# A tiled softmax: eight rows of the sixth chunk loaded on ScalarE's DMA queue, and all row scaling on VectorE one row at a time

## The chip, the cores and the metric

The kernel runs on one core of one Trainium2 chip. The metric is device time in microseconds of that core. Three runs of the kernel before took 161.74 to 161.76 us, with a median of 161.75 us.

## The reference

The input `x` is 16 x 1024 rows of 512 float32 values. The output is a softmax over each row with temperature 0.5:

```python
x_scaled = x / 0.5
x_max = np.max(x_scaled, axis=-1, keepdims=True)
exp_x = np.exp(x_scaled - x_max)
return (exp_x / np.sum(exp_x, axis=-1, keepdims=True)).astype(np.float32)
```

That is 33.55 MB to read from device memory and 33.55 MB to write back.

## The kernel before

The 16,384 rows are cut into eight chunks of 2048 rows. A chunk is one tile `xt` of 128 partitions with 16 rows each, so each partition holds 16 x 512 floats (32 KB, contiguous in device memory), and a chunk is 4 MB. Six buffers hold six chunks. Chunks 6 and 7 (counted from 0, as in the code) reuse the buffers of chunks 0 and 1. Everything is done in place.

A chunk is worked on as one or more blocks (`BLOCKS`): chunk 0 in blocks of 4, 4 and 8 rows, chunk 7 in two of 8 rows, the others whole. This gives eleven blocks. For one block the steps are:

- `load` (line 68): a DMA on SyncE's (SP's) queue. Chunk 0 comes in two parts (1 MB and 3 MB), chunks 1 to 6 whole, and chunk 7 without its last row per partition.
- `shift` (lines 77 and 81): VectorE takes the negated maximum of every row in one reduction and doubles it; this is the bias.
- `exponentials` (line 108): ScalarE takes each row's exponential with that bias in one activation, and the sum of the row beside it (`accum_out`, a second instruction in the trace).
- `scale_vector` (lines 125 and 127): VectorE takes the reciprocals of the sums and multiplies seven eighths of the rows by them in one broadcast tensor-tensor product (14 of 16 rows; of a 4-row block, all).
- `scale_scalar` (line 138): ScalarE multiplies the remaining rows one by one with a copy activation (two rows of a whole chunk, one of an 8-row block).
- `store` (line 148): a DMA on ScalarE's queue writes the whole chunk (4 MB).

The order on each engine is the order in which the program issues it, written out by hand in the loop at the end. Step `i` issues the exponentials of block `i+1`, then the scaling of block `i`, then the load and the maximum of block `i+2`, then the store of block `i`. Chunk 1 is an exception: its last two exponentials come behind the store of chunk 0 (`cut`). The last row per partition of chunk 7 is loaded by GpSimd (`load_last_row`, lines 90 and 97) once the exponentials of chunk 5 have reached row 10.

A DMA is carried by 16 DMA engines. Each takes 8 of the 128 partitions, so a whole-chunk transfer is 8 packets of 32 KB on each engine. The trace calls SP's queue q1, ScalarE's q10, GpSimd's q0, and the one that fetches instructions q14.

Of the kernel before, what the change touches and what calls it, by code (L numbers as in the profile page):

```python
# [1 line left out]

# [4 lines left out]


@with_exitstack
def kernel(  # L10
    ctx: ExitStack,
    tc: tile.TileContext,
    x: bass.AP,
    out: bass.AP,
):
    nc = tc.nc
    fp32 = mybir.dt.float32
    P = nc.NUM_PARTITIONS
    AX = mybir.AxisListType.X
    EXP = mybir.ActivationFunctionType.Exp  # L20
    COPY = mybir.ActivationFunctionType.Copy
    MAX = mybir.AluOpType.max

    D = x.shape[-1]
    xf = x.flatten_outer_dims()
    of = out.flatten_outer_dims()
    N = xf.shape[0]

    G = 16
    C = N // (P * G)
    assert C * P * G == N
    xr = xf.rearrange("(c p g) d -> c p g d", p=P, g=G)
    outr = of.rearrange("(c p g) d -> c p g d", p=P, g=G)
    WHOLE = [(0, G)]
    LOADS = [[(0, 4), (4, G)]] + [WHOLE] * 6 + [[(0, G - 1)]]
    BLOCKS = [[(0, 4), (4, 8), (8, G)]] + [WHOLE] * 6 + [[(0, 8), (8, G)]]
    STORES = [WHOLE] * 8  # L40
    BMAX = 16
    BUFS = 6

    data = ctx.enter_context(tc.tile_pool(name="data", bufs=BUFS))
    stats = ctx.enter_context(tc.tile_pool(name="stats", bufs=6))

    ctx.enter_context(tc.manual_schedule())


    warm = stats.tile([P, 1], fp32, name="warm", bufs=1)  # L50
    nc.vector.memset(warm, 0.0)  # L51
    nc.scalar.activation(out=warm, in_=warm, func=EXP)  # L52

    chunks = {}
    blocks = [(c, lo, hi) for c in range(C) for lo, hi in BLOCKS[c]]
    n = len(blocks)
    biases, sums, recips = {}, {}, {}

    finished = []

    def load(c):
        if c < BUFS:
            chunks[c] = data.tile([P, G, D], fp32, name="xt")
        else:
            chunks[c] = chunks[c - BUFS]
        xt = chunks[c]
        for lo, hi in LOADS[c]:
            part = nc.sync.dma_start(out=xt[:, lo:hi, :], in_=xr[c][:, lo:hi, :])  # L68
            finished.append(part.ins.name)

    def shift(i):
        c, lo, hi = blocks[i]
        if c not in chunks:
            load(c)
        b = hi - lo
        negmax = stats.tile([P, BMAX], fp32, name="negmax")
        nc.vector.tensor_reduce(  # L77
            negmax[:, 0:b], chunks[c][:, lo:hi, :], axis=AX, op=MAX, negate=True
        )
        biases[i] = stats.tile([P, BMAX], fp32, name="bias")  # L80
        nc.vector.tensor_scalar_mul(biases[i][:, 0:b], negmax[:, 0:b], 2.0)  # L81

    def load_last_row(signal):
        seen = stats.tile([P, 1], fp32, name="seen", bufs=1)
        copied = nc.gpsimd.tensor_copy(out=seen, in_=signal)  # L90
        finished.append(copied.ins.name)
        c = C - 1
        halves = "p (h d) -> p h d"
        to = chunks[c - BUFS][:, G - 1, :].rearrange(halves, h=2)
        of_ = xr[c][:, G - 1, :].rearrange(halves, h=2)
        for p0, p1 in ((P - 2, P), (0, P - 2)):
            part = nc.gpsimd.dma_start(  # L97
                out=to[p0:p1], in_=of_[p0:p1], max_dma_last_dim=2 * D
            )
            finished.append(part.ins.name)  # L100

    def exponentials(i, rows):
        c, lo, hi = blocks[i]
        if i not in sums:
            sums[i] = stats.tile([P, BMAX], fp32, name="sums")
        for g in rows:
            row = chunks[c][:, lo + g, :]
            nc.scalar.activation(  # L108
                out=row,
                in_=row,  # L110
                func=EXP,
                bias=biases[i][:, g : g + 1],
                scale=2.0,
                accum_out=sums[i][:, g : g + 1],
            )
            if c == BUFS - 1 and g == 10:
                load_last_row(sums[i][:, g : g + 1])


    def scale_vector(i):  # L120
        c, lo, hi = blocks[i]
        b = hi - lo
        k = b - b // 8
        recips[i] = stats.tile([P, BMAX], fp32, name="recip")
        nc.vector.reciprocal(recips[i][:, 0:b], sums[i][:, 0:b])  # L125
        rows = chunks[c][:, lo : lo + k, :]
        last = nc.vector.tensor_mul(  # L127
            rows, rows, recips[i][:, 0:k].unsqueeze(2).broadcast_to((P, k, D))
        )
        if i == n - 1:  # L130
            finished.append(last.ins.name)

    def scale_scalar(i):
        c, lo, hi = blocks[i]
        b = hi - lo
        for g in range(b - b // 8, b):
            row = chunks[c][:, lo + g, :]
            last = nc.scalar.activation(  # L138
                out=row, in_=row, func=COPY, scale=recips[i][:, g : g + 1]
            )  # L140
            if i == n - 1:
                finished.append(last.ins.name)

    def store(i):
        c, _, end = blocks[i]
        for lo, hi in STORES[c]:
            if hi == end:
                part = nc.scalar.dma_start(
                    out=outr[c][:, lo:hi, :], in_=chunks[c][:, lo:hi, :]
                )  # L150
                if c < C - 1:
                    finished.append(part.ins.name)

    shift(0)
    shift(1)

    def rows(i):
        c, lo, hi = blocks[i]
        cut = hi - lo - (2 if c == 1 else 0)
        return range(cut), range(cut, hi - lo)  # L160

    exponentials(0, rows(0)[0])
    for i in range(n):
        if i + 1 < n:
            exponentials(i + 1, rows(i + 1)[0])
        scale_vector(i)
        scale_scalar(i)
        if i + 2 < n:
            shift(i + 2)
        store(i)  # L170
        if i + 1 < n:
            exponentials(i + 1, rows(i + 1)[1])

    seen = nc.sync.nop()
    info = mybir.DependencyInfo(
        mybir.DependencyClass.Sync, mybir.DependencyReason.DATA
    )
    for name in finished:
        tc.add_manual_dep(seen.ins, name, info, reason="leaves one wait for the end")


# [1 line left out]
_INS = ['x']  # L183
_OUTS = [((16, 1024, 512), 'float32')]


# [23 lines left out]
```

## Time and profile before

| What | Value |
|---|---|
| Runs, median (lowest to highest) | 161.75 us (161.74 to 161.76) |
| Span of the profiled execution | 160.5 us |
| VectorE (DVE) busy | 134.6 us, 84% of the span |
| ScalarE (ACT) busy | 102.2 us, 64% of the span |
| Moved by DMA | 67.13 MB, mean 418 GB/s |
| Time of SP's and ScalarE's packets, as a share of the 16 DMA engines' span | 49.3% and 48.4% |
| First and last store issued | at 44.1 and 147.5 us |

The profiled execution lists its span, and no total of its own beside it. The runs' median lies 1.24 us above the span, which is what lies around the span: start and end of the program. Times in the trace count from the start of the span. Busy shares are averages; the share in one stretch is read from the slices and windows of the profile. A packet is put down to the slice in which it starts, so a single short slice can show more or less than the DMA engines moved in it.

### The profile page before, as it was taken

The numbers are of one execution on the slowest core, as the hardware profiler recorded it, in microseconds if no ns is written. First come the engines' busy times: TensorE is split into PE (matmuls) and PEld (weight loads), VectorE is DVE, ScalarE is ACT, GpSimd is POOL, SyncE is SP. The second block draws the span as 40 slices with busy tenths as digits, with TensorE's granted clock in tenths as the row PEclk, the third lists the DMA queues.
The fourth block names the chain that finished last, engine by engine and source line by source line (L and its number), as shares of the span: only waits on it lengthen the run. The fifth ranks groups of instructions, "written<-read, shape, count | busy, mean of one in ns | idle before, by whom it ended". The sixth has DMA issues, their size and how long they took to land.

```text
span 160.5 us, 411 instructions
## 1 busy us (share of the span) xinstructions
DVE 134.6 (84%) x45; ACT 102.2 (64%) x273; POOL 1.9 (1%) x7
## 2 busy tenths in 40 slices
DVE  0607999999999999999999999999999999957000
ACT  3071549069989963998199909991899891790000
POOL 0000000000000000000000000030000000000000
DMA  5999999999989999999999999989999999999994
GB/s 184 470 408 498 400 392 457 457 392 402 506 269 425 490 392 400 506 400 392 490 425 392 474 434 392 490 383 483 422 450 400 400 465 441 392 457 449 400 441 204
DMA packets 2578, 67.13 MB, mean 418 GB/s; under 512 B 328, under 2 KB 328, under 8 KB 400
## 3 DMA queue, kind: packets, MB, share of 16 engines
q1 hardware_dynamic: 1296, 33.29, 49.3%
q10 hardware_dynamic: 1152, 33.55, 48.4%
q0 software_dynamic: 128, 0.26, 0.4%
q14 instruction: 2, 0.02, 0.0%
HBM read 33.55 MB, written 33.55 MB: 418 GB/s over the span
## 4 chain that ended last, share of the span: by engine, by line
DVE 75%; DMA 7%; issue 5%; ACT 3%; SPq 0%
DVE negmax L77 42%; DVE xt L127 31%; DMA xt<-in_x_dram 7%; ACT xt L108 3%; DVE bias L81 1%; DVE recip L125 1%; SPq L68 0%
## 5 line engine op out<-in xcount | busy, mean ns | idle before, releaser
L108 ACT ACTIVATE xt<-xt,bias 128x512 f32<-128x512 f32 x128 | 90.4, 708 | 41.5 <-DVE bias L81 40.6
L77 DVE TENSOR_REDUCE negmax<-xt 128x16 f32<-128x8192 f32 (+2 forms) x11 | 69.9, 6352 | 9.4 <-DMA xt<-in_x_dram 9.4
L127 DVE TENSOR_TENSOR xt<-xt,recip 128x7168 f32<-128x7168 f32 (+2 forms) x11 | 62.0, 5637 | 0.4
L108 ACT ACTIVATION_READ_ACCUMULATOR xt<-xt,bias 128x1 f32 x128 | 23.9, 187 | 0.0
L138 ACT ACTIVATE xt<-xt,recip 128x512 f32<-128x512 f32 x15 | 9.9, 706 | 0.0
L125 DVE RECIPROCAL recip<-sums 128x16 f32<-128x16 f32 (+2 forms) x11 | 2.4, 218 | 1.8 <-ACT xt L108 1.8
L81 DVE TENSOR_SCALAR bias<-negmax 128x16 f32<-128x16 f32 (+2 forms) x11 | 1.9, 173 | 0.4
L52 ACT ACT_TABLE_LOAD x1 | 1.3, 1283 | 0.7 <-PEq L194 0.7
L97 POOL DMA_DIRECT2D xt<-in_x_dram x2 | 1.5, 741 | 0.5 <-issue 0.5
L90 POOL COPY seen<-sums 128x1 f32<-128x1 f32 x1 | 0.2, 184 | 103.6 <-ACT xt L108 103.6
L51 DVE MEMSET warm<- 128x1 f32 x1 | 0.1, 59 | 0.8 <-PEq L194 0.8
L52 ACT ACTIVATE warm<-warm 128x1 f32<-128x1 f32 x1 | 0.2, 202 | 0.0
L194 POOL MEMSET const-float32-0.0<- 128x1 f32 x1 | 0.1, 93 | 0.2 <-issue 0.2
L194 POOL MEMSET const-bfloat16-1.0<- 128x1 bf16 x1 | 0.1, 95 | 0.0
L194 POOL MEMSET const-uint8-127<- 128x1 uint8 x1 | 0.1, 95 | 0.0
L194 POOL MEMSET const-float32-1.0<- 128x1 f32 x1 | 0.1, 93 | 0.0
## 6 DMA issues: line engine op xcount, KB each, us to landing
out_dram<-xt ACTq DMA_DIRECT2D x8, 4096.0 KB, 23.1
xt<-in_x_dram SPq DMA_DIRECT2D x6, 4096.0 KB, 34.8
xt<-in_x_dram SPq DMA_DIRECT2D x1, 3840.0 KB, 27.8
xt<-in_x_dram SPq DMA_DIRECT2D x1, 3072.0 KB, 11.6
xt<-in_x_dram SPq DMA_DIRECT2D x1, 1024.0 KB, 4.8
xt<-in_x_dram POOLq DMA_DIRECT2D x1, 252.0 KB, 15.4
xt<-in_x_dram POOLq DMA_DIRECT2D x1, 4.0 KB, 9.1
```

The costliest lines, as they stand in the source:

```text
L51: nc.vector.memset(warm, 0.0)
L52: nc.scalar.activation(out=warm, in_=warm, func=EXP)
L77: nc.vector.tensor_reduce(negmax[:, 0:b], chunks[c][:, lo:hi, :], axis=AX, op=MAX, negate=True)
L81: nc.vector.tensor_scalar_mul(biases[i][:, 0:b], negmax[:, 0:b], 2.0)
L90: copied = nc.gpsimd.tensor_copy(out=seen, in_=signal)
L97: part = nc.gpsimd.dma_start(out=to[p0:p1], in_=of_[p0:p1], max_dma_last_dim=2 * D)
L108: nc.scalar.activation(out=row, in_=row, func=EXP, bias=biases[i][:, g : g + 1], scale=2.0, accum_out=sums[i][:, g : g + 1],)
L125: nc.vector.reciprocal(recips[i][:, 0:b], sums[i][:, 0:b])
L127: last = nc.vector.tensor_mul(rows, rows, recips[i][:, 0:k].unsqueeze(2).broadcast_to((P, k, D)))
L138: last = nc.scalar.activation(out=row, in_=row, func=COPY, scale=recips[i][:, g : g + 1])
L194: nc = _bacc.Bacc("TRN2", target_bir_lowering=False, num_devices=1)
```

## The change

There are three edits.

First, directly behind the table load and the warm-up activation, ScalarE issues a load of rows 0 to 7 of chunk 5 (the sixth) on its own queue, ahead of all stores. `max_dma_last_dim` cuts each partition's 16 KB into four pieces of two rows (4 KB). SP's queue then loads only rows 8 to 15 of that chunk.

Second, `scale_scalar` is gone. VectorE scales every row with a tensor-scalar product of its own (128 x 512), with the row's reciprocal as the scalar.

Third, the store of chunk 0 is issued after 12 of the 16 exponentials of chunk 1, not after 14.

```diff
-    LOADS = [[(0, 4), (4, G)]] + [WHOLE] * 6 + [[(0, G - 1)]]
+    SLOW = 8
+    LOADS = [[(0, 4), (4, G)]] + [WHOLE] * 4 + [[(SLOW, G)], WHOLE, [(0, G - 1)]]
...
+    def load_slowly(c):
+        chunks[c] = data.tile([P, G, D], fp32, name="xt")
+        part = nc.scalar.dma_start(
+            out=chunks[c][:, 0:SLOW, :],
+            in_=xr[c][:, 0:SLOW, :],
+            max_dma_last_dim=2 * 4 * D,
+        )
+        finished.append(part.ins.name)
+
+    load_slowly(BUFS - 1)
...
     def load(c):
-        if c < BUFS:
+        if c in chunks:
+            pass
+        elif c < BUFS:
             chunks[c] = data.tile([P, G, D], fp32, name="xt")
...
-        if c not in chunks:
+        if lo == 0:
             load(c)
...
-    def scale_vector(i):
+    def scale(i):
         c, lo, hi = blocks[i]
         b = hi - lo
-        k = b - b // 8
         recips[i] = stats.tile([P, BMAX], fp32, name="recip")
         nc.vector.reciprocal(recips[i][:, 0:b], sums[i][:, 0:b])
-        rows = chunks[c][:, lo : lo + k, :]
-        last = nc.vector.tensor_mul(
-            rows, rows, recips[i][:, 0:k].unsqueeze(2).broadcast_to((P, k, D))
-        )
+        for g in range(b):
+            row = chunks[c][:, lo + g, :]
+            last = nc.vector.tensor_scalar_mul(row, row, recips[i][:, g : g + 1])
         if i == n - 1:
             finished.append(last.ins.name)
-
-    def scale_scalar(i):
...
-        cut = hi - lo - (2 if c == 1 else 0)
+        cut = hi - lo - (4 if c == 1 else 0)
         return range(cut), range(cut, hi - lo)
...
-        scale_vector(i)
-        scale_scalar(i)
+        scale(i)
```

In the changed program's order, SP's load of the rest of chunk 5 waits for the semaphore of ScalarE's load of its first rows, and the loads of chunks 6 and 7 stand behind it on SP. The exponentials of chunk 5 wait for both of these loads.

More of the change, by code (lines that the diff above doesn't have):

```diff
@@ L20 @@
     EXP = mybir.ActivationFunctionType.Exp
-    COPY = mybir.ActivationFunctionType.Copy
     MAX = mybir.AluOpType.max
@@ L54 @@
     chunks = {}
+    finished = []
+    def load_slowly(c):
[7 more added lines that the diff above has]
+    load_slowly(BUFS - 1)
     blocks = [(c, lo, hi) for c in range(C) for lo, hi in BLOCKS[c]]
@@ L57 @@
     biases, sums, recips = {}, {}, {}
-    finished = []
     def load(c):
-        if c < BUFS:
+        if c in chunks:
+            pass
+        elif c < BUFS:
             chunks[c] = data.tile([P, G, D], fp32, name="xt")
@@ L117, in exponentials @@
                 load_last_row(sums[i][:, g : g + 1])
-    def scale_vector(i):
+    def scale(i):
         c, lo, hi = blocks[i]
         b = hi - lo
-        k = b - b // 8
         recips[i] = stats.tile([P, BMAX], fp32, name="recip")
         nc.vector.reciprocal(recips[i][:, 0:b], sums[i][:, 0:b])
-        rows = chunks[c][:, lo : lo + k, :]
-        last = nc.vector.tensor_mul(
-            rows, rows, recips[i][:, 0:k].unsqueeze(2).broadcast_to((P, k, D))
-        )
+        for g in range(b):
+            row = chunks[c][:, lo + g, :]
+            last = nc.vector.tensor_scalar_mul(row, row, recips[i][:, g : g + 1])
         if i == n - 1:
             finished.append(last.ins.name)
-    def scale_scalar(i):
[L134 to L142, printed above, removed]
     def store(i):
```

## The prediction

> **What bounds the kernel now.** I read the chain of waits first, and it misleads: it blames VectorE.
>
> ```profile
> span 160.5 us, 411 instructions
> DVE 134.6 (84%) x45; ACT 102.2 (64%) x273; POOL 1.9 (1%) x7
> DVE 75%; DMA 7%; issue 5%; ACT 3%; SPq 0%
> ```
>
> The DMA slices and queues below say otherwise. The DMA engines are busy in every slice but the first and the last, and the two hardware queues' packets fill 49.3 + 48.4 = 97.7% of their time.
>
> ```profile
> DMA  5999999999989999999999999989999999999994
> GB/s 184 470 408 498 400 392 457 457 392 402 506 269 425 490 392 400 506 400 392 490 425 392 474 434 392 490 383 483 422 450 400 400 465 441 392 457 449 400 441 204
> q1 hardware_dynamic: 1296, 33.29, 49.3%
> q10 hardware_dynamic: 1152, 33.55, 48.4%
> ```
>
> Single slices jitter, so I asked for long windows, and then for short ones around the low slice (269). Columns: stretch, length, busy time of VectorE, ScalarE, GpSimd, TensorE clock, DMA share, GB/s.
>
> ```profile
> 2.00:44.00 42.00, 33.45 (x15) 22.35 (x63) 0.00 (x0) 1.00 1.01 432
> 44.00:50.00 6.00, 5.93 (x4) 5.28 (x16) 0.00 (x0) 1.00 0.98 344
> 50.00:118.00 68.00, 67.72 (x17) 51.97 (x141) 1.66 (x3) 1.00 1.00 433
> 118.00:158.00 40.00, 27.44 (x11) 21.35 (x56) 0.00 (x0) 1.00 1.01 434
> ...
> 47.00:48.00 1.00, 1.00 (x1) 1.00 (x5) 0.00 (x0) 1.00 0.26 98
> ```
>
> Loads alone, loads with stores, and stores alone all run at 432 to 434 GB/s. 67.11 MB at 433 is 155.0 us, and the first packet starts at 1.74, so the span is nearly all transfer. The one flaw is 44 to 50 us: 6 x (1 - 344/433) = 1.23 us lost, edges included. The first store is issued at 44.10, its first packet starts at 48.41. In the packet records, load packets of 32 KB that normally take 1.213 us took up to 2.49 there. Their excess sums to 17.3 us over 16 engines, or **1.08 us each**. I use that figure and call it the hitch.
>
> How far is VectorE from binding? Its last product ends at 147.39, and the last store is issued at 147.48. The store before it still has packets until 149.51. A transfer starts 1.0 us after its issue (first load: 0.74 to 1.74). So VectorE is covered by 149.51 - 148.48 = **1.0 us**: the DMA engines decide the end, and a faster VectorE alone brings nothing.
>
> **Part 1, the scaling.** Rows of the trace:
>
> ```profile
> L127 DVE TENSOR_TENSOR xt<-xt,recip 128x7168 f32<-128x7168 f32 x6 | 45.7, 7625 | 0.2
> L127 DVE TENSOR_TENSOR xt<-xt,recip 128x2048 f32<-128x2048 f32 x2 | 4.6, 2292 | 0.1
> L138 ACT ACTIVATE xt<-xt,recip 128x512 f32<-128x512 f32 x15 | 9.9, 706 | 0.0
> L81 DVE TENSOR_SCALAR bias<-negmax 128x16 f32<-128x16 f32 x6 | 1.0, 174 | 0.2
> L81 DVE TENSOR_SCALAR bias<-negmax 128x4 f32<-128x4 f32 x2 | 0.3, 170 | 0.1
> ```
>
> Eleven products disappear. VectorE's next instruction starts 0.09 us before one ends, so they cost 6 x 7.53 + 3 x 3.80 + 2 x 2.20 = 61.0 us. They become 128 row products. No row shows a tensor-scalar of 512 elements. Upper bound: the product's slope, (7625 - 2292)/5120 = 1.04 ns per element, gives 0.53 + 0.16 fixed - 0.09 = 0.60 us a row. Lower bound: the bias row, the same operation, grows by 4 ns over 12 elements, 0.33 ns each, so 0.17 + 0.17 - 0.09 = 0.25 us. I take the middle of the lower half, 0.34, as the operation is that of the bias row: 43.5 us, 17.5 less. VectorE binds only if 128t exceeds 61.0 + 1.0 cover - 1.9 (its later start, part 2), that is above t = 0.47 us. Below that, this part is worth 0: what is late next is the load of chunk 7, which lands at 115.3.
>
> The Trainium skill, "VectorE: DVE Perf Modes", section "The perf-mode tier table", lists fp32 tensor_tensor in SBUF at single speed (2293 ns for 2048 elements; the row here has 2292) and tensor_scalar at double (1227 ns), which no run here shows; an estimate from it is 0.34 us a row, so no cost.
>
> ScalarE loses 15 copies of 0.706 us. It waits 40.6 us for the bias in all, so that is worth nothing, except that the stores go out sooner.
>
> **Part 2, the slow load.** The data moved stays the same. In chunk 5, each DMA engine gets 32 packets of 4 KB and 8 of 16 KB in place of 8 of 32 KB. 4 KB take 0.159 us (packet records of GpSimd's last-row load). 32 x 0.159 - 4 x 1.213 = 0.24, and some 0.03 for the 16-KB packets and one more semaphore: **+0.27 us**, on the path.
>
> Delay at the start: in 52 to 54 us, records of both queues alternate packet for packet. If ScalarE's load, issued at 2.2, joins at 3.3 to 5, chunk 0 is whole up to 12 pieces x 0.159 = 1.9 us later, and VectorE with it. DMA stays full, so this costs 0. SP's second half of chunk 5 waits for ScalarE's load, and behind it stand the loads of chunks 6 and 7. The cover is chunk 4, which SP's queue still carries until 57.2; ScalarE's load must land before that. Counting pieces against SP's packets (8 per transfer, one piece after each), the 32nd goes out between 36.5 and 44 us, so the cost is 0. Without the cover SP's queue would stand empty from 57.2 until that landing, and before the first store the engines would idle for as long.
>
> Why it may gain: both queues are then in use during the loads, before any store. The question is what the hitch is. Two single 8-KB packets of the instruction queue (q14, at 37.7 and 97.1) have a companion row: the next load packet on their engine took 0.165 and 0.246 us too long. The disturbance thus goes with the size of the packet that joins: an 8-KB packet takes 0.31, a 32-KB store packet 1.21, and the hitch is 1.08. A 4-KB joiner would cost at most 0.16. If the store queue is still live when chunk 0's store reaches it, the store joins nothing new. That store now goes out behind 12 exponentials instead of 14 and a copy: some 42.5 to 43.5 us, against the slow load's end at 36.5 to 44. It is close, but this is the likelier reading: -1.08 + 0.16 + 0.27 = **-0.65 us**.
>
> The Trainium skill, "DMA: Bandwidth & Descriptors", section "Issuing engines are not separate DMA queues", speaks against it: starting DMAs from several engines at once only saves issue time. By that the sum is +0.27, or 162.0 us; the stretch 44 to 50 at 344 GB/s is a row it does not explain.
>
> **Part 3, the store after 12 exponentials.** 2 x 0.705 us earlier on ScalarE, alongside VectorE's longer work; it only matters for the joining above.
>
> **Sum.** Against the span: 160.51 - 0.65 = 159.9; 1.24 us lie around it (161.75 - 160.51). Forecast 161.1 us.
>
> **Rivals.**
> 1. *The hitch stays whole.* It belongs to the first store itself or to the first use of the queue (then it is moved to 3 to 6 us), or the slow load ends before the store comes. For it: the windows show only one first store, which is also the queue's first use, so they can't part the two. Against: the stretched load packets beside the 8-KB fetches. Time 161.75 + 0.27 = 162.0 us.
> 2. *The hitch comes twice*, once when the slow load joins and again when the store does, after the queue has run dry. 161.75 + 1.08 + 0.27 = 163.1 us.
> 3. *VectorE becomes the bound* (the slower side). Mechanism: a row product at single speed, in the 128 instructions of the new scaling. Price: 128 x 0.60 = 76.8, so +15.8, +1.9 later start, -1.0 cover: 161.75 + 16.7 = 178.4 us. It decides from t = 0.47 us a row. Against: the bias rows hardly grow.
> 4. *The change doesn't do what it says*: the four pieces of a partition go as one 16-KB packet. Then the slow load is over by 12 to 17 us, the store joins a dead queue, and it is case 1.
>
> **How the numbers follow.** Something under 0.2% (0.32 us) cannot be told from no change: 161.43 to 162.07 is "same". Gain as forecast: 0.55, all of it faster. Hitch kept (1 and 4): 0.25, at 162.0 near the edge of same, so 0.17 same and 0.08 slower. Hitch twice: 0.10, slower. VectorE bound: 0.05, slower. The other 0.05 I split between same (0.02) and slower (0.03). Faster 0.55, same 0.19, slower 0.26.
>
> Range: the forecast's own is 160.6 (the hitch gone, no price for joining, and a little less of the excess of load packets at 19 to 40 us, 0.2 us per engine) to 161.4. To hold 8 in 10 it must reach over the kept hitch to 162.0, and to the double one, 163.1, as 0.55 + 0.25 is only just 0.8. The VectorE case is left out. Range 160.6 to 163.1.
>
> **What would show it.** Right: no window between 40 and 50 us near 344 GB/s, first store's packets soon after its issue, DMA full from 2 to 158, row products of about 0.43 us, VectorE done near 140 us and still no gain from that. Wrong: a low slice at 3 to 6 us or at the first store (rivals 1 and 2), ScalarE's load landing before 20 us (4), row products near 0.69 us and DMA idle late (3).

## The result and the profile after

The changed kernel takes 166.43 us (165.28 to 166.67 in four runs) against 161.75 us: **slower, ratio 1.0272, interval 1.0242 to 1.0301**. The forecast was 161.1 us in a range of 160.6 to 163.1, so it missed both the direction and the range.

The head of the page after, with the DMA slices and the chain of waits:

```profile
span 164.9 us, 509 instructions
DVE 124.7 (76%) x162; ACT 92.9 (56%) x258; POOL 1.9 (1%) x7
...
DMA  5999999999999999989999999999999999992885
GB/s 197 427 441 418 432 429 437 429 445 415 374 501 392 421 461 390 493 378 433 429 429 485 390 437 447 398 462 395 432 460 412 413 453 398 390 437 87 382 382 254
...
DMA 59%; DVE 24%; ACT 8%; issue 1%; SPq 0%; DVEq 0%
```

VectorE has ten microseconds less work (134.6 to 124.7), ScalarE nine. The DMA line carries the news: the last four slices read 2, 8, 8, 5 where 9, 9, 9, 4 stood. The first of them moved 87 GB/s. The windows of the changed kernel (columns as before) place the gap:

```profile
40.00:44.00 4.00, 4.00 (x1) 4.00 (x13) 0.00 (x0) 1.00 1.05 385
44.00:50.00 6.00, 5.93 (x11) 5.19 (x15) 0.00 (x0) 1.00 1.01 437
50.00:118.00 68.00, 59.01 (x71) 42.85 (x121) 1.66 (x3) 1.00 1.00 430
...
148.00:154.00 6.00, 3.46 (x9) 1.33 (x4) 0.00 (x0) 1.00 0.43 186
...
150.00:152.00 2.00, 2.00 (x7) 0.00 (x0) 0.00 (x0) 1.00 0.04 16
```

Up to 118 us the transfers run about as fast as before. The stretch with a lower rate, where the first store begins, now lies at 40 to 44 us (385 GB/s). Between 148 and 154 us the DMA engines are idle more than half of the time, and between 150 and 152 us almost wholly, while VectorE finishes the last chunk. From the packet records, a budget per DMA engine, kernel before and after:

- packets at their usual duration: 155.59 and 155.89 us (+0.30)
- stretched packets, start included: 1.94 and 1.79 us (-0.15)
- idle between first and last packet, as what is left: none and 4.21 us (+4.2)

The sum, +4.4, is the growth of the span (160.5 to 164.9). So the loss is idle time at the end. About 4 us of it lie before the last store's packets. About half a microsecond lies at 139 to 140 us, before the packets of chunk 6's store, which was issued only at 138.98. Why it arises shows in two issue rows (first the changed kernel's, then that of the kernel before; the last figure is the time from issue to landing) and in VectorE's waits for loads (total, times, longest; the changed kernel's first):

```profile
xt<-in_x_dram SPq DMA_DIRECT2D x1, 3840.0 KB, 47.3
```

```profile
xt<-in_x_dram SPq DMA_DIRECT2D x1, 3840.0 KB, 27.8
```

```profile
DVE negmax L89 <- DMA xt<-in_x_dram: 24.0, 6, 6.3
```

```profile
DVE negmax L77 <- DMA xt<-in_x_dram: 9.4, 2, 4.8
```

The load of chunk 7 takes 47.3 us from issue to landing where it took 27.8. It is issued 7.6 us sooner (80.4 against 88.0) and lands 12 us later. VectorE now waits six times for loads, 24.0 us in all; before it waited twice, 9.4 us. The timeline of the end shows what hangs on that landing (start, duration, engine, line; in brackets the idle time before):

```profile
127.71 4.42 DVE L89 TENSOR_REDUCE negmax<-xt 128x8 f32<-128x4096 f32 x1 [3.70 <-DMA xt<-in_x_dram]
...
132.53 6.42 DVE L139 TENSOR_SCALAR xt<-xt,recip 128x512 f32<-128x512 f32 x16
...
138.87 4.41 DVE L89 TENSOR_REDUCE negmax<-xt 128x8 f32<-128x4096 f32 x1
...
149.60 3.26 DVE L139 TENSOR_SCALAR xt<-xt,recip 128x512 f32<-128x512 f32 x8
...
152.89 0.34 ACTq L147 DMA_DIRECT2D out_dram<-xt  x1
```

From the last load packet of chunk 7 (126.0 in the packet records; 114.1 before) to the last store's issue there are 27 us of maximum, exponentials and scaling, and another 10.7 us to the last packet. Chunk 6 hangs on it too, since VectorE takes the maximum of chunk 7's first half ahead of chunk 6's scaling. Before, VectorE reached chunk 7 only at 120.5. With the 1.7 us that lie between the last packet and the maximum in the changed kernel (126.0 to 127.71), that load had some 5 us to spare. The last row, which GpSimd loads, is in at 128.4 and holds nothing up: it belongs to the second half, whose maximum starts at 138.87.

Why do the loads come late? **Loads and stores take turns, packet for packet.** While both queues have work, the records show as many packets of one as of the other: 24.1 load and 24.7 store packets per DMA engine from 52 to 110 us before, 33.1 and 33.9 from 45 to 122 us in the changed kernel. A load packet of 1.21 us is followed by a store packet of 1.21 us, so each load packet still to come when the stores begin costs about 2.43 us. Per DMA engine 26 load packets were left at that moment in the kernel before, 35 in the changed one (8 of them of 16 KB). With 30-KB packets for chunk 7 (1.138 us) that counts to 49.9 + 18 x 2.43 + 8 x 2.35 = 112.4 us, and 43.2 + 19 x 2.43 + 8 x 1.82 + 8 x 2.35 = 122.7 us. (The sums start when the first store's packets run on the DMA engines; 1.82 and 2.35 us are a 16-KB or 30-KB load packet and a store packet.) Measured: 114.1 and 126.0. The count gives 10 of the 12 us.

Two things raise the number. The slow load puts 5 us of its own packets between SP's. And the first store goes out earlier, at 38.93 instead of 44.10:

```profile
38.81 0.71 ACT L120 ACTIVATE xt<-xt,bias 128x512 f32<-128x512 f32 x1
38.93 0.36 ACTq L147 DMA_DIRECT2D out_dram<-xt  x1
```

That is the seventh exponential of chunk 1, and the store stands behind the twelfth in ScalarE's program. It waits for no computation of ScalarE any more, only for VectorE's last product of chunk 0, which had ended 1.0 us before (37.93). Before, it waited for ScalarE's own copy to be finished.

### The profile page after: what moved, and what is told of

Read it like the earlier page. It is cut to its first block, busy times and chain, and to the rows that moved or that the text cites. A ratio compares the mean times of both kernels' runs of the same rounds, so it can differ in the third digit from the quotient of the medians.

```text
span 164.9 us, 509 instructions
## 1 busy us (share of the span) xinstructions
DVE 124.7 (76%) x162; ACT 92.9 (56%) x258; POOL 1.9 (1%) x7
## 4 chain that ended last, share of the span: by engine, by line
DMA 59%; DVE 24%; ACT 8%; issue 1%; SPq 0%; DVEq 0%
DMA xt<-in_x_dram 43%; DMA out_dram<-xt 16%; DVE negmax L89 16%; ACT xt L120 8%; DVE xt L139 7%; SPq L80 0%; DVE recip L136 0%; DVE bias L93 0%; DVEq L203 0%
## 5 line engine op out<-in xcount | busy, mean ns | idle before, releaser
L120 ACT ACTIVATE xt<-xt,bias 128x512 f32<-128x512 f32 x128 | 90.4, 708 | 55.6 <-DVE bias L93 25.8
L89 DVE TENSOR_REDUCE negmax<-xt 128x16 f32<-128x8192 f32 (+2 forms) x11 | 69.9, 6356 | 24.1 <-DMA xt<-in_x_dram 24.0
L139 DVE TENSOR_SCALAR xt<-xt,recip 128x512 f32<-128x512 f32 x128 | 51.7, 480 | 0.4
## 6 DMA issues: line engine op xcount, KB each, us to landing
xt<-in_x_dram SPq DMA_DIRECT2D x1, 3840.0 KB, 47.3
```

What stands on the lines that cost most here:

```text
L89: nc.vector.tensor_reduce(negmax[:, 0:b], chunks[c][:, lo:hi, :], axis=AX, op=MAX, negate=True)
L120: nc.scalar.activation(out=row, in_=row, func=EXP, bias=biases[i][:, g : g + 1], scale=2.0, accum_out=sums[i][:, g : g + 1],)
L139: last = nc.vector.tensor_scalar_mul(row, row, recips[i][:, g : g + 1])
```

## The experiments

The theory (A): the last chunk lands too late, because stores start sooner and the slow load pushes SP's loads back; past a limit the DMA engines run dry. The limit, an estimate: transfers alone end near 159.2, minus 10.7 minus 27, so chunk 7's last packet must be in by about 121.5. Rivals: the row products cost by themselves (B), or the slow load alone does (C).

One table for all; times in us. "Left" is the number of load packets per DMA engine when the stores begin, "in" is the last load packet of SP's queue, "idle" the idle time per DMA engine between its first and last packet.

| Kernel | first store issued | left | in | last store issued | idle | time |
|---|---|---|---|---|---|---|
| before | 44.1 | 26.1 | 114.1 | 147.5 | 0 | 161.75 |
| changed | 38.9 | 35.0 | 126.0 | 152.9 | 4.2 | 166.43 |
| scaling only | 37.9 | 31.2 | 120.1 | 147.3 | 0 | 162.41 |
| slow load only | 46.0 | 29.1 | 119.5 | 149.4 | 1.3 | 163.80 |
| changed, first store held | 47.0 | 28.0 | 116.9 | 143.8 | 0 | 163.46 |
| changed, half store packets | 39.2 | 34.0 | 111.4 | 140.8 | 0 | 163.31 |
| changed, last store split | 39.3 | 34.3 | 124.1 | 151.2 | 0 | 163.23 |
| scaling only, first store held | 44.6 | 25.8 | 113.2 | 140.0 | 0 | 162.81 |

The kernel before ran at 161.85 beside the first four experiments and at 161.91 beside the others.

**Scaling only.** From the changed kernel, without the slow load, and with the old cut:

```diff
-    LOADS = [[(0, 4), (4, G)]] + [WHOLE] * 4 + [[(SLOW, G)], WHOLE, [(0, G - 1)]]
+    LOADS = [[(0, 4), (4, G)]] + [WHOLE] * 6 + [[(0, G - 1)]]
...
-    load_slowly(BUFS - 1)
...
-        cut = hi - lo - (4 if c == 1 else 0)
+        cut = hi - lo - (2 if c == 1 else 0)
```

> Only the row scaling of the change; all loads on SP's queue, the store of chunk 0 behind 14 exponentials. Theory A (turns of the queues): the stores no longer wait for ScalarE's copies and go out about 5 us sooner, each load packet then shares with a store packet earlier, so chunk 7 lands about 5 us later than before (near 121), which the 25 us from there to the last store's issue still allow: 161.5 to 162.0 us. Theory B (the row products themselves cost, by holding something that the loads or GpSimd need): about 165 to 166 us, with chunk 7 landing near 127.

162.41 us, ratio 1.0031 (1.0021 to 1.0042). The store goes out 6.2 us sooner, chunk 7 is in 6.0 us later, within the limit, and the end has no gap:

```profile
148.00:154.00 6.00, 0.00 (x0) 0.00 (x0) 0.00 (x0) 1.00 1.01 437
```

The row products alone don't cost 4.7 us, so B falls as the cause. The 0.4 us over theory A's range stays open (below).

**Slow load only.** From the changed kernel, the scaling of the kernel before (`scale_vector` and `scale_scalar`, whose definitions come back), and the old cut:

```diff
-        scale(i)
+        scale_vector(i)
+        scale_scalar(i)
...
-        cut = hi - lo - (4 if c == 1 else 0)
+        cut = hi - lo - (2 if c == 1 else 0)
```

> Only the slow load of the change; scaling as before, the store of chunk 0 behind 14 exponentials and a copy. Theory A: the first store goes out near 46, chunk 7 lands near 115 to 117, VectorE starts 1.8 us late and ends near 149, past its cover of 1.0 us: 162.1 to 162.9 us. Theory C (the slow load alone costs it all, by its small packets or by pushing SP's loads back): 165 to 166 us.

163.80 us, ratio 1.0126 (1.0102 to 1.0149): between the two figures, 0.9 over A's. So C gives 2.0 of the 4.7 us and not all. The trace shows the cause that A named, VectorE's late start (it waits 1.9 us longer for the loads of chunk 0), only without room for it. The last product ends 1.9 us later, at 149.3, and the store before has just run out:

```profile
149.00:151.00 2.00, 0.29 (x1) 0.00 (x0) 0.00 (x0) 1.00 0.61 262
```

1.3 us of idle time there and 0.28 us for the smaller packets make most of the 2.0 us. Chunk 7 was in at 119.5, later than expected (115 to 117), but here VectorE reached it at 122.4 anyway. Note that the two parts push chunk 7 back by 6.0 and 5.4 us alone and by 11.9 us together: the lateness adds up, but the loss does not (0.6 and 2.0 us alone, 4.7 together), as a limit would have it. The third edit, the store behind 12 exponentials instead of 14, is in neither kernel, and no run has it alone. By the length of two exponentials it brings the first store forward by 1.4 us, an estimate.

**Changed, first store held.** Only chunk 0's store is moved, behind four exponentials of chunk 2 (`HELD = 2` is the block whose store it is):

```diff
-        if i + 1 < n:
+        if i == HELD + 1:
+            exponentials(i + 1, range(0, 4))
+            store(HELD)
+            exponentials(i + 1, range(4, 16))
+        elif i + 1 < n:
             exponentials(i + 1, rows(i + 1)[0])
...
-        store(i)
+        if i != HELD:
+            store(i)
```

> The changed kernel, with the store of chunk 0 held back behind all exponentials of chunk 1 and the first four of chunk 2 (issued near 47 in place of 38.9); nothing else moved. Theory A: about as many load packets are left as before when the stores start, chunk 7 lands near 115 to 117, the DMA engines don't run dry at the end: 161.6 to 162.4 us. Theories B and C: no change from the changed kernel, 165 to 166.7 us.

163.46 us, ratio 1.0095 (1.0074 to 1.0116). A store issued 8 us *later* makes the kernel 3.0 us faster. Seven load packets fewer are left, chunk 7 is in at 116.9, and the gap is gone:

```profile
148.00:154.00 6.00, 0.00 (x0) 0.00 (x0) 0.00 (x0) 1.00 1.01 437
```

It stays 1.1 us above A's range. No gap is left; one DMA engine ends 0.7 us after the others.

**Changed, half store packets.** Issue order unchanged; the stores of chunks 0 to 3 take turns with half the size:

```diff
                     out=outr[c][:, lo:hi, :], in_=chunks[c][:, lo:hi, :],
+                    **(dict(max_dma_last_dim=8 * 4 * D) if c < 4 else {}),
```

> The changed kernel, with the stores of chunks 0 to 3 cut into packets of 16 KB in place of 32 KB; issue order and all else unchanged. Theory A (loads and stores take turns packet for packet, and the last chunk lands too late): each turn of a store is half as long, chunk 7 lands 10 us or more earlier than its 127 us, the DMA engines have no gap at the end, 161.8 to 163.0 us in spite of some 0.3 us for more packets. Rival (the idle time at the end comes from the early stores themselves or from GpSimd's late last row, not from where chunk 7 lands): 165 to 167 us.

163.31 us, ratio 1.0082 (1.0062 to 1.0102). Almost as many load packets are left as in the changed kernel (34.0), yet chunk 7 is in 14.6 us sooner. That is the direct test of the turns: from 46 to 88 us the records still show about as many load packets as store packets (24.9 and 27.0 per DMA engine), so with store packets of half the size the loads got the larger share of the bytes. The price is 0.59 us of packet time against the kernel before (156.18 against 155.59), and stores that finish later: SP's load of chunk 7, which needs the buffer of chunk 1, is issued at 91.9 instead of 80.4. The time is 0.3 over the range; the gap is gone, so the rival falls: the store is as early as in the changed kernel.

**Changed, last store split.** The loads stay late, only the end is cut up:

```diff
-    STORES = [WHOLE] * 8
+    STORES = [WHOLE] * 7 + [[(0, 8), (8, G)]]
```

> The changed kernel, with the last chunk stored in two halves, the first as soon as its rows are scaled. Chunk 7 still lands near 127. Theory A: the loss is the stretch in which the DMA engines wait for the last scaling; a half store fills it, and behind the last scaling only 2 MB are left (4.9 us less): 162.0 to 163.5 us. Rival (the loss lies in the loads or in the row products, before the end): 165.5 to 167 us.

163.23 us, ratio 1.0089 (1.0056 to 1.0122), as A expected. Chunk 7 is in at 124.1, past the limit, but half of it is stored at once and fills the gap:

```profile
148.00:154.00 6.00, 3.16 (x8) 0.00 (x0) 0.00 (x0) 1.00 0.96 412
```

So three edits that have only the gap in common (an earlier landing twice, a filled gap once) each take back 3.0 to 3.2 us of the 4.7. The 1.3 to 1.6 us that these three kernels keep over the kernel before are not the gap. Of these, 0.3 to 0.6 us are packet time.

**Scaling only, first store held.** Both edits above, without the slow load.

> Only the row scaling, all loads on SP's queue, and the store of chunk 0 held behind the first four exponentials of chunk 2 (issued near 46). Theory A: the same order of loads and stores as in the kernel before, chunk 7 lands near 115 to 118, 161.7 to 162.2 us, no gain from 10 us less work on VectorE. If the row products cost by themselves: 162.4 us or more, as with the scaling alone.

162.81 us, ratio 1.0054 (1.0035 to 1.0073). Loads and stores are in the same order as before (25.8 left, in at 113.2), VectorE is through by 140, and still nothing is gained. It is 0.6 above A's range and nominally meets B's small figure. In the packet records 15 of 16 DMA engines end by 159.19, as before (159.11), and one at 160.05. A late last engine stands in four more profiles: with the slow load alone, the store held, half packets and the split store, the last one ends 0.6 to 0.9 us after the second last, against 0.1 in both profiles of the kernel before. The slow load alone has the old scaling, so row products aren't needed for it. Where that one loses its time isn't settled, so a cost of the row products of 0.5 to 0.9 us can't be excluded; it would not be in the packets, whose usual duration sums to 155.61 as before.

**A small first store.** The kernel before, with chunk 0's rows 0 and 1 stored ahead on their own:

```diff
-    STORES = [WHOLE] * 8
+    STORES = [[(0, 2), (2, G)]] + [WHOLE] * 7
...
-            if hi == end:
+            if end == G:
```

> The kernel before, with the store of chunk 0 led by a store of its rows 0 and 1 alone (4-KB packets), the other 14 rows behind it. If the hitch goes with the size of the packet that joins: most of the 1.08 us is gone, no low stretch between 44 and 50 us, 160.7 to 161.2 us. If it belongs to the first store or to the first use of the queue: 161.7 to 161.9 us.

163.31 us, ratio 1.0085 (1.0068 to 1.0102): slower, and neither expectation holds. The 4-KB packets join with 0.1 us of stretched packets, but when the 28-KB packets follow on the same queue, which is still live, the stretch comes (the hitch, as the prediction calls it): 0.9 us between 52 and 60 us. Another 1.0 us comes at 84 to 88, just before the packets of chunk 2's store. So the hitch isn't tied to the queue's first use or to its having run dry. Its cause stays open.

**The kernel before, again.**

> The kernel before, unchanged, for a second profile: 161.7 to 162.2 us. If the 1.08 us of stretched load packets at the first store are a fixed price of that store, they are found again; if they vary from execution to execution, as 0.5 to 0.7 us in the runs so far suggest, the sum is lower and the span nearer 160.0 than 160.5 us.

161.97 us, ratio 1.0003 (0.9989 to 1.0017). This profiled execution took 161.94 us with a span of 160.16, so 1.78 us lie around a span, not 1.24. The 1.24 came from setting the span of one execution against the median of others. By 1.78, the first profile's execution, with its 160.5 us, took about 162.3 us. The forecast takes no harm from it, since 1.24 is taken off the time before and added again. The hitch is there again:

```profile
44.00:50.00 6.00, 5.93 (x4) 5.27 (x16) 0.00 (x0) 1.00 1.00 355
```

By packet records it is 1.08 us here too (0.95 at 44 to 48, 0.13 at 48 to 52). Around the first whole store, the load packets' stretch sorts by the slow load: 0.9 to 1.1 us per DMA engine in the four profiles without it (before twice, the scaling alone, the scaling with the store held), 0.5 to 0.7 in the five with it (0.67 in the changed kernel).

## Why the prediction was wrong

- **"The DMA engines decide the end, and a faster VectorE alone brings nothing"**: right. Ten microseconds less work on VectorE gained nothing in either kernel with the scaling alone. In the changed kernel itself they no longer decide the end alone: they stood idle for 4.2 us.
- **The row product, 0.34 us, from 0.25 to 0.60**: measured (6.42 - 0.48)/15 = 0.40 us from start to start. It lies in the bounds and below the 0.47 from which VectorE binds, so rival 3 did not happen. The sum fell from 61.0 to 51, not to 43.5.

```profile
L139 DVE TENSOR_SCALAR xt<-xt,recip 128x512 f32<-128x512 f32 x128 | 51.7, 480 | 0.4
```

- **Packets, +0.27 us**: measured +0.30.
- **"DMA stays full, so this costs 0"** and **"what is late next is the load of chunk 7, which lands at 115.3"**: here the prediction failed. The DMA engines did not stay full: they idled for 4.2 us, because chunk 7's last load packet came at 126.0 and not, as in the old trace, at 114.1. I took the landing of chunk 7 from the old trace and kept it. The same paragraph used the turns, packet for packet, to find the end of the slow load, and did not follow them to the last load. The rule of the count above could be read in the trace before. Its start, the first store's packets at 43.2, could not be had from my store time, so the next point is part of the same miss. With a landing near 123 plus 27 to the last store and 10.7 behind it, the last packet ends at 160.4, already a loss; with the 126.0 that came, at 163.7.
- **The first store "some 42.5 to 43.5 us"**: it went out at 38.93. I assumed that ScalarE issues a DMA when the instructions ahead of it have run. That held before, since the store waited for the copy. Removing the copies removed this wait: I wrote "except that the stores go out sooner" and priced it at nothing. How much hangs on it shows in the kernel with the store held, the same loads and scaling: a store at 47.0 has chunk 7 in at 116.9, one at 38.9 has it in at 126.0. Between the two, a store at 43 gives 121.4, an estimate, and that is just the limit.
- **The slow load's own path**: its last packet was expected to go out between 36.5 and 44 and did at 39; right. Its small packets did stay separate, so rival 4 did not happen.
- **The hitch, -1.08 + 0.16**: only part of it went. Around the first store the load packets are stretched by 0.67 us where it was 1.08, so the gain was 0.4 us and not 0.9. That makes 0.5 us of the miss, and the case lies between the forecast and rival 1. A smaller hitch goes with the slow load in all profiles (above); why isn't tested. The reading from the 8-KB fetches (the stretch goes with the joining packet) fits the 4-KB store that joined with 0.1 us. What it was used for, that a store joins nothing new on a live queue, fell with the small first store. Rival 2 did not happen: at 4.4 us, when the slow load joins, nothing is stretched.
- **The Trainium skill**, "DMA: Bandwidth & Descriptors", section "Issuing engines are not separate DMA queues", spoke against the change, and the runs agree that a second queue brought no bandwidth (426 GB/s between 8 and 36 us with the slow load, 431 before). Its sum, 162.0, was nearer than mine. The loss of 4.7 us is not in that rule: the second queue and the earlier store changed which transfers come first.

I had named idle DMA late in the kernel as a sign of rival 3 only. It came with row products of 0.40 us, under the 0.47 from which VectorE binds.

## What to carry to other kernels

When the DMA engines are the bound, follow the order of the transfers to the very last load, and ask what work hangs behind it: a store that goes out sooner takes turns from loads, and the bytes it moves early are missing at the end, where they would have covered the last chunk's work. The two queues here got shares by packet size, so count packets and not megabytes. Before a step is taken off an engine, list what waited for it: such a wait can be what holds the order.

## What was not expected of the hardware

- ScalarE issued a DMA ahead of its own computations where none of them was waited for: the store stood behind twelve exponentials and went out during the seventh, and behind fourteen during the ninth with the scaling alone (37.94), five ahead both times. The slow load was issued at 0.91 us, during the table load (0.74 to 2.02).
- The first packet of the slow load came 3.5 us after its issue (0.91 to 4.38), and the first store's 3.5 to 4.6 us over the ten profiles, against 1.0 us for SP's first load and 0.8 us for the changed kernel's last store, whose issue found the DMA engines idle.
- Halving the store packets brought the last load in by 14.6 us, with 0.3 us more of packet time than the changed kernel.
